# Forgetting heads' values as seven half-block products, logits and rotary key beside 256 latent columns, three gate pairs ahead

## The chip, the cores and the metric

One core of a Trainium2 chip runs the kernel. The metric is the device time of one execution in microseconds (us). Engines: TensorE (PE) for matmuls, VectorE (DVE), ScalarE (ACT), GpSimd (POOL) and SyncE (SP); SP and POOL also issue the DMA transfers, each into its own queue.

## The reference

512 tokens, width 2048, 16 heads of width 128, one input projection of 6472 columns. Cut to what matters:

```
h = _rms_norm(x, g_pre)
q_lat, kv_lat, k_rope_raw, gate_mla, fq, fk, fv, f_logit, gate_fox = split(h @ w_in)
# widths 768, 512, 64, 1024, 1024, 1024, 1024, 8, 1024
o_mla = _mla_branch(rms(q_lat) @ w_uq, rms(kv_lat) @ w_ukv, rope(k_rope_raw)) * silu(gate_mla)
# forgetting heads: c = cumsum(log_sigmoid(f_logit + b_forget))
# logits = q k^T * scale + c_q - c_k, causal softmax, times fv
o_fox = _fox_branch(fq, fk, fv, f_logit, b_forget) * silu(gate_fox)
return x + _rms_norm(concatenate([o_mla, o_fox]) @ w_out, g_post)
```

`fv` is the value projection (1024 columns, 8 heads), `f_logit` the forget logits (8 columns), `k_rope_raw` the rotary key (64 columns), and `q_lat` with `kv_lat` the latents (1280 columns).

## The kernel before

**Numbers.** Each operand is split into a high and a low part, and `mm3` (L139) makes a product of three matmuls: high by high, high by low, low by high. x normalised and transposed lies in SBUF as 16 k-tiles of 128 rows (`hh`, `hl`; `h0` to `h15` in the trace). Weights come in chunks of up to 128 x 1024, loaded by SP (`load`, tile `raw`); `divide` (L255) lets ScalarE make `whi` and VectorE `wlo`, always two chunks ahead of TensorE; the load of a chunk is issued four ahead (`chunk`, L275). Three `raw`, three `whi` and three `wlo` buffers rotate.

**Stages in order.** The list of chunks sets the order.
1. `proj_first` transposes x and multiplies each k-tile at once, with 456 columns: the values of three forgetting heads, 8 logits, 64 of the rotary key.
2. Four pairs of forgetting heads: for pair p the queries `fq`, keys `fk`, (pairs 1 and 2) the values `fv`, and the gates `fg`, each 256 columns: 96 matmuls of 512 tokens with the weights stationary (`proj_T`), while values have the tokens stationary and the weight columns moving (`proj_V`). Pair 1 makes two heads' values (256 wide), pair 2 three (384 wide). `todo` is a list of small steps (attention blocks, fetches); each k-tile of a projection runs one (`pump`). Scores of a pair run beside its gates, values beside the next pair's queries.
3. `lat`: the last 256 latent columns, 96 matmuls of 512.
4. The other 1024 latent columns (group "l") and the 1024 gate columns of the latent heads (group "m"), each as seven products of half blocks (`p1`, `p2`, `p4`, `q6`, `g5`, `g7`, `g3`; 8 k-tiles, 48 matmuls of 512) in place of eight.
5. The latent heads in four pairs ("MLA"), then the output product, again in seven products per half ("o").

**What the half-block products need.** (a) Sums of weight blocks (`t7`, `t6`, `t4`, `t5`), made in DRAM by the DMA engines: `add_step` copies the first block (SP) and adds the second with an accumulating DMA (POOL). `paced` does one step for every so many k-tiles (`pace` 6; a step is 512 KB copied and 512 KB added). A step starts once a mark, written from a weight tile in use, has landed. A late sum (`t4` of l and m, `t5` of o) is not made: its second block is loaded beside the first (`second`) and added by VectorE in `join` (L248). (b) Sums and differences of x's two halves: `x_steps` (L997) adds high and low part (`xr`), `away_steps` (L900) subtracts (`rmg`) and POOL writes the results to DRAM; `fetches` reads them back, `divisions` splits them. These x steps run in `later`, one in three k-tiles, from pair 1 on.

## Time and profile before

| | |
|---|---|
| median of 3 runs | 908.48 us (908.34 to 908.54) |
| the profiled execution, and its span | 905.47 us, 903.7 us |
| TensorE, VectorE, ScalarE, POOL busy | 99%, 70%, 48%, 8% |
| moved by DMA | 195.20 MB, mean 216 GB/s |
| DMA queues: q1 (loads by SP), q0 (POOL) | 55.0% and 20.6% of 16 engines |

Busy time of TensorE counts pipelined matmuls, each modelled as longer than the distance to the next one, so the distances matter more than the 99%. In the row of 40 slices one slice is 22.6 us. In the timeline's rows stand start, duration, engine, tile, line and operation; in the rows of waits tile and line, what released it, total us, count, mean us; in rows of groups the busy time, mean ns of one, and idle time before.

### The profile page before, as it was taken

Reading aid. Unit: us, or ns where it says so; the run is one execution under the profiler, and the core shown is the slowest. Engines: PE = TensorE matmul, PEld = TensorE weight load, DVE = VectorE, ACT = ScalarE, POOL = GpSimd, SP = SyncE. Lnnn points to the kernel's source line nnn. Section 1 sums busy time; section 2 is a strip of 40 time slices with the busy share of each in tenths; the row PEclk is TensorE's granted clock in tenths of the full one; section 3 lists DMA queues with packets and bytes.
Section 4 is the critical chain, followed back from the end, with each engine's and each line's share of the span. In section 5 each row is a group of like instructions: output and inputs, shape, how many; then the busy total and the mean of one; then the engine's idle time right before and its main releaser. Section 6 shows DMA issues by size and latency. Waiting matters only on the chain.

```text
span 903.7 us, 12931 instructions
## 1 busy us (share of the span) xinstructions
PE 895.0 (99%) x4730; PEld 773.2 (86%) x4730; DVE 630.6 (70%) x1070; ACT 433.4 (48%) x806; POOL 71.6 (8%) x89
## 2 busy tenths in 40 slices
PE   9999999999999999999999999999999999999996
PEld 8888888898889988888998998888889888888885
DVE  4477778537463684474867778858879895997785
ACT  6772434234222342233456556545565576645383
POOL 1010102110120110111100000000100000000021
PEclk9999999999999999999999999999999999999999
DMA  9377988987897798988998865247863146798878
GB/s 304 96 202 195 255 203 203 242 228 186 232 262 200 193 245 221 235 218 207 335 396 307 276 212 164 59 109 187 175 171 118 48 139 205 244 320 322 253 222 250
DMA packets 120195, 195.20 MB, mean 216 GB/s; under 512 B 15906, under 2 KB 59452, under 8 KB 120132
## 3 DMA queue, kind: packets, MB, share of 16 engines
q1 hardware_dynamic: 106052, 158.84, 55.0%
q0 software_dynamic: 13344, 35.13, 20.6%
q8 instruction: 37, 0.61, 0.3%
q10 hardware_dynamic: 736, 0.40, 0.2%
q14 instruction: 26, 0.21, 0.1%
HBM read 182.27 MB, written 62.41 MB: 271 GB/s over the span
## 4 chain that ended last, share of the span: by engine, by line
PE 95%; DMA 2%; DVE 1%; ACT 0%; issue 0%; SPq 0%; ACTq 0%; DVEq 0%
PE fv L581 4%; PE fg L140 3%; PE fq L142 3%; PE fq L140 3%; PE fq L141 3%; PE fg L142 3%; PE fg L141 3%; PE fk L141 3%; PE fk L140 3%; PE fk L142 3%; PE sm L624 3%; PE fv L140 2%; PE fv L142 2%; PE fv L141 2%; PE mq L140 2%; PE mq L142 2%
## 5 line engine op out<-in xcount | busy, mean ns | idle before, releaser
L265 DVE TENSOR_TENSOR wlo<-raw,whi 128x1024 fp32r<-128x1024 f32 (+3 forms) x205 | 242.4, 1186 | 157.7 <-ACT whi L262 154.2
L262 ACT CAST whi<-raw 128x1024 fp32r<-128x1024 f32 (+3 forms) x205 | 208.9, 1022 | 287.1 <-PE fk L141 52.9
L140 PE MATMUL fq<-h,whi 128*128 128x512 f32 x128 | 52.6, 411 | 0.0
L140 PE MATMUL fg<-h,whi 128*128 128x512 f32 x128 | 50.9, 398 | 0.0
L142 PE MATMUL fq<-h,wlo 128*128 128x512 f32 x128 | 50.4, 393 | 0.0
L141 PE MATMUL fq<-h,whi 128*128 128x512 f32 x128 | 50.1, 392 | 0.0
L142 PE MATMUL fg<-h,wlo 128*128 128x512 f32 x128 | 50.1, 391 | 0.0
L140 PE MATMUL fk<-h,whi 128*128 128x512 f32 x128 | 50.0, 391 | 0.0
L141 PE MATMUL fg<-h,whi 128*128 128x512 f32 x128 | 49.9, 390 | 0.0
L142 PE MATMUL fk<-h,wlo 128*128 128x512 f32 x128 | 49.8, 389 | 0.0
L141 PE MATMUL fk<-h,whi 128*128 128x512 f32 x128 | 49.8, 389 | 0.0
L142 PE MATMUL fv<-whi,h 128*128 128x256 f32 (+1 forms) x128 | 39.5, 309 | 0.0
L141 PE MATMUL fv<-wlo,h 128*128 128x256 f32 (+1 forms) x128 | 39.5, 309 | 0.0
L140 PE MATMUL fv<-whi,h 128*128 128x256 f32 (+1 forms) x128 | 39.5, 309 | 0.0
L581 PE MATMUL fv<-whi,h 128*128 128x456 f32 x128 | 38.0, 380 | 0.0
L314 POOL DMA_DIRECT2D t<-t x16 | 13.4, 836 | 303.2 <-DMA t<-in_w_out_dram 266.5
L646 ACT ACTIVATE pf<-sf,stf 128x128 f32<-128x128 f32 (+3 forms) x32 | 16.9, 529 | 26.9 <-DVE stf L639 26.9
L140 PE MATMUL mq<-ln,whi 128*128 128x512 f32 x72 | 29.0, 402 | 0.0
L142 PEld LDWEIGHTS fq<-h,wlo 128*128 128x128 f32 x128 | 24.0, 188 | 5.4
L142 PEld LDWEIGHTS fg<-h,wlo 128*128 128x128 f32 x128 | 24.0, 188 | 5.3
L142 PEld LDWEIGHTS fk<-h,wlo 128*128 128x128 f32 x128 | 24.0, 188 | 5.0
L140 PEld LDWEIGHTS fk<-h,whi 128*128 128x128 f32 x128 | 24.0, 188 | 4.9
(519 smaller groups left out, 2471.2 us busy)
## 6 DMA issues: line engine op xcount, KB each, us to landing
raw<-in_w_in_dram SPq DMA_DIRECT2D x80, 512.0 KB
raw<-in_w_out_dram SPq DMA_DIRECT2D x32, 512.0 KB
t<-in_w_out_dram SPq DMA_DIRECT2D x24, 512.0 KB
raw<-t SPq DMA_DIRECT2D x24, 512.0 KB
t<-t POOLq DMA_DIRECT2D x16, 512.0 KB, 7.8
awaymg<-rmg POOLq DMA_DIRECT2D x8, 512.0 KB, 8.0
t<-in_w_out_dram POOLq DMA_DIRECT2D x8, 512.0 KB, 8.2
raw<-t6l SPq DMA_DIRECT2D x8, 512.0 KB
```

Source lines behind the costliest of these rows:

```text
L140: pe.matmul(o, ah, bh, start=first, stop=False, **kw)
L141: pe.matmul(o, ah, bl, start=False, stop=False, **kw)
L142: pe.matmul(o, al, bh, start=False, stop=last, **kw)
L262: cast = act.copy(hi[:, :m], raw[:, :m])
L265: dve.tensor_tensor(out=lo[:, :m], in0=raw[:, :m], in1=hi[:, :m].bitcast(F32), op=ALU.subtract)
L314: pool.dma_start(to.rearrange("p (k c) -> p k c", k=2), second, accum_op=ALU.add)
L581: pe.matmul(banks[t][:, :n], a[k][:, tss[t]], b[:, j, :], start=k == 0 and m == 0, stop=k == NK - 1 and m == 2,)
L624: pe.matmul(s[:, :nn], a[:, qs], c[:, :nn], start=(i == 0), stop=(i == len(pairs) - 1))
L646: act.activation(p, s[:, :n], AF.Exp, bias=st[:, 0:1], scale=unit, accum_out=st[:, 1:2])
```

## The change

1. `proj_first` multiplies 328 columns: the last 256 latent columns, the 64 of the rotary key, the 8 logits. The latent columns are written to DRAM (`l4_away`), fetched after pair 3's scores and transposed (8 transposes); product `lat` goes.
2. The values of all 8 forgetting heads become group "v" of the seven products. `t4` and `t5` of v are late sums (joins on VectorE), `t7` and `t6` eight steps of the planner. Results are combined by `scaled` and `scaled_copy` with the tokens' scale, written to DRAM by POOL (`v_out`, eight writes of half a unit of 512 KB), and fetched and split per pair (`load_v`, `split_v`).
3. The gates of pairs 0, 1 and 2 come ahead: g0, p1, g1, p2, g5, g2, g3, q0, q6, g7, p4, k0, q1, k1, q2, k2, q3, k3, g3 of pair 3. Scores of a pair now run beside the next pair's queries, values beside its keys; the last pair's values beside product `p1` of l.
4. The x steps run right after the first stage as ordinary steps of `todo`; rotary tables and key after the fetched operands of `g5` are split. `later`, `behind`, `proj_V` and `fox_v` go.
5. `pace` is 7 instead of 6; v's sums stand first in the list, then l and m; the output sums are 1024 columns wide (1 MB copied, 1 MB added; 12 steps for 24), and a wide step takes twice the k-tiles. In the latent heads the pace is 1.45 instead of 3. `out_cols` permutes the output's column blocks to fit. `needs` holds at build time that a sum is issued before the chunk that reads it.
6. A pool `vr` (five buffers) holds the blocks of v, two of five `raw` tiles and `second` in this part; `pp` (attention tiles) opens after the block of values; the deep pool of weight buffers, which opened ahead of product `p1` of l, opens after it.

```
-V3 = 3 * HW
+L4 = KVR // 2
+KL = L4 + ROPE
...
     def raw_tile(i):
         if deep and deep[1] <= i < deep[2] and (i - deep[1]) % (DEEP + 3) < DEEP:
             return deep[0].tile([P, 1024], F32, tag="raw", name=f"raw{i}", bufs=DEEP)
+        if i <= prods["p4", "v"][-1] and i % 5 < 2:
+            return vr.tile([P, 1024], F32, tag="raw", name=f"raw{i}", bufs=2)
...
-    state = {"loaded": 0, "divided": 0, "tiles": 0, "turn": 0, "step": -1, "pace": 6}
+    state = {"loaded": 0, "divided": 0, "tiles": 0, "step": -1, "pace": 7}
...
-    fox = []
-    for p in range(4):
-        c = {}
-        if p == 0:
-            c["v"] = add_chunks(
-                w_in, [(0, O_FV + 5 * HW, V3 + NH), (V3 + NH, O_KR, ROPE)], NK, 2, V3 + ROPE + NH, single=2
-            )
-        at = 256 * (3 - p)
-        c["q"] = add_chunks(w_in, [(0, O_FQ + at, 256)], NK, 4, 256)
-        c["k"] = add_chunks(w_in, [(0, O_FK + at, 256)], NK, 4, 256)
-        if p == 1:
-            c["v"] = add_chunks(w_in, [(0, O_FV + 3 * HW, 2 * HW)], NK, 4, 2 * HW)
-        if p == 2:
-            c["v"] = add_chunks(w_in, [(0, O_FV, V3)], NK, 2, V3)
-        c["g"] = add_chunks(w_in, [(0, O_GF + at, 256)], NK, 4, 256)
-        fox.append(c)
-    lat = add_chunks(w_in, [(0, 1024, 256)], NK, 4, 256)
...
-    AT = {"l": 0, "m": O_GM}
+    AT = {"v": O_FV, "l": 0, "m": O_GM}
...
-    for g in "lm":
-        sum_blocks(g, lambda j, h, c, g=g: in_block(g, j, h, c), "t4")
+    for g in "vlm":
+        sum_blocks(g, lambda j, h, c, g=g: in_block(g, j, h, c), ("t4", "t5") if g == "v" else ("t4",))
...
+    first = add_chunks(w_in, [(0, O_KR - L4, KL), (KL, O_F, NH)], NK, 2, KL + NH, single=2)
+    fox = [{} for _ in range(4)]
+    for n in ("g0", "p1", "g1", "p2", "s5", "g2", "s3", "q0", "s6", "s7", "p4", "k0",
+              "q1", "k1", "q2", "k2", "q3", "k3", "g3"):
+        name = {"p1": "p1", "p2": "p2", "p4": "p4", "s5": "g5", "s3": "g3", "s6": "q6", "s7": "g7"}.get(n)
...
+    sum_blocks("o", lambda j, h, c: out_block((K1, K2)[h][j], slice(1024 * c, 1024 * (c + 1))), ("t5",), 1024)
...
+            wide = 0 <= state["step"] < len(bg) and bg[state["step"]][0].shape[1] > 1024
+            pace = state["pace"] * (1 + wide)
...
+    for j in range(4):
+        todo.extend(x_steps(j))
+    wait(4)
+    todo.extend(fetches("g5", "m"))
+    todo.extend(divisions("g5", "m"))
+    todo.append(lambda: todo.extendleft(reversed([*rotary_tables(), rotary_key])))
+
+    fox_g(0, [att_bank("fg00"), bank("pv", "fg01", 1)])
+    A = two_of(proj_bank, "va")
+    product("p1", "v", x_block(0, 0), A, True, True)
+    pa, pb = v_block("vpa"), v_block("vpb")
+    scaled_copy(pa, A, 0, rcol)
+    scaled_copy(pb, A, 2, rcol)
+    fox_g(1, two_of(proj_bank, "fg1"))
+    product("p2", "v", x_block(1, 0), A, False, True)
+    c11 = v_block("vc11")
+    scaled_copy(c11, A, 0, rcol)
+    v_out(c11, 0, 0)
+    drain()
+    G = two_of(att_bank, "vg")
+    product("g5", "v", operand("g5", "m"), G, True, True)
...
+    B = two_of(proj_bank, "vp4")
+    product("p4", "v", x_block(1, 2), B, True, True)
+    scaled(c21, B, 2, c21, col=rcol)
+    v_out(c21, 1, 0)
...
-    todo.append(rotary_key)
-    set_pace(4)
     lb = [proj_bank(f"l4{i}") for i in range(2)]
-    proj_T(lat, [(lb[i], P, two[i]) for i in range(2)], hh, hl)
-    while later:
-        later.popleft()()
     for i in range(2):
+        for t in range(NT):
+            pe.transpose(lb[i][:, t * P : (t + 1) * P], l4[:, t, i * P : (i + 1) * P], ident)
         latent(8 + i, lb[i])
...
+    set_pace(1000)
+    A, A2 = ([proj_bank(f"g{n}{t}") for t in range(2)] for n in "lm")
+    product("p1", "l", x_wide(0, 0), A, True, True, 2, turned=True)
+    drain()
     heads_room.close()
...
-            set_pace(3)
+            set_pace(1.45)
```

In the rows of the order, tile names carry a running number; `rf`, `fz`, `fw`, `fd` belong to the forget sums, `gf` and `ghf` to the gates, `nk` to the forget keys, `fqt` to the queries.

VectorE, up to the split of the chunk that TensorE needs about 140 matmuls after the first stage; first before:

```order
L748 TENSOR_TENSOR fw_773<-fw_773,fz_772 8x512
L749 TENSOR_SCALAR fd_774<-fw_773 8x512
L750 TENSOR_TENSOR fd_774<-fd_774,fz_772 8x512
L751 TENSOR_TENSOR fw_773<-fw_773,fd_774 8x512
L1022 SCALAR_TENSOR_TENSOR fqt00_893<-fq00_728,rrow_211 128x512
L753 SCALAR_TENSOR_TENSOR fz_772<-fz_772,fw_773 8x512
L1022 SCALAR_TENSOR_TENSOR fqt01_899<-fq01_729,rrow_211 128x512
L754 SCALAR_TENSOR_TENSOR rf_215<-fz_772,fd_774 8x512
L132 TENSOR_TENSOR fq00_895<-fqt00_893,fq00_895 128x384
L132 TENSOR_TENSOR fq01_901<-fqt01_899,fq01_901 128x384
L265 TENSOR_TENSOR wlo15_924<-raw15_830,whi15_923 128x1024
L265 TENSOR_TENSOR wlo16_957<-raw16_862,whi16_956 128x1024
```

and after the change:

```order
L749 SCALAR_TENSOR_TENSOR rf_215<-fz_762,fd_764 8x512
L1000 TENSOR_TENSOR xr01_878<-h3_309 128x512
L1000 TENSOR_TENSOR xr11_879<-h10_483 128x512
L1000 TENSOR_TENSOR xr11_879<-h11_515 128x512
L692 SCALAR_TENSOR_TENSOR ghf6_905<-fg00_718,rrow_211 128x512
L692 SCALAR_TENSOR_TENSOR ghf7_909<-fg01_719,rrow_211 128x512
L272 TENSOR_TENSOR wlo15_918<-raw15_826,whi15_917 128x1024
L914 TENSOR_TENSOR rmg51_927<-xr01_878,xr11_879 128x512
L694 SCALAR_TENSOR_TENSOR gf0_904<-gf0_904,ghf6_905 128x512
L694 SCALAR_TENSOR_TENSOR gf0_904<-gf0_904,ghf7_909 128x512
L914 TENSOR_TENSOR rmg51_927<-xr01_878,rmg51_927 128x512
L272 TENSOR_TENSOR wlo16_941<-raw16_866,whi16_940 128x1024
```

The x sums (`xr`, `rmg`) now stand among the splits of the chunks.

TensorE at the third chunk of the product that follows the first one of the list (before: keys of pair 0, after: `p1` of v), before:

```order
L140 MATMUL fk00_919<-h8_418,whi15_923 128x512
L141 MATMUL fk00_919<-h8_418,whi15_923 128x512
L142 MATMUL fk00_919<-h8_418,wlo15_924 128x512
L140 MATMUL fk01_920<-h8_418,whi15_923 128x512
L141 MATMUL fk01_920<-h8_418,whi15_923 128x512
L142 MATMUL fk01_920<-h8_418,wlo15_924 128x512
```

and after:

```order
L142 MATMUL va0_913<-whi15_917,h4_333 128x512
L142 MATMUL va1_914<-whi15_917,h4_333 128x512
L142 MATMUL fg10_1012<-h0_243,whi17_963 128x512
L143 MATMUL fg10_1012<-h0_243,whi17_963 128x512
L142 MATMUL fg11_1013<-h0_243,whi17_963 128x512
L143 MATMUL fg11_1013<-h0_243,whi17_963 128x512
L143 MATMUL va0_913<-wlo15_918,h4_333 128x512
L144 MATMUL va0_913<-whi15_917,h4_333 128x512
L143 MATMUL va1_914<-wlo15_918,h4_333 128x512
L144 MATMUL va1_914<-whi15_917,h4_333 128x512
```

Matmuls that need only `whi`, four of them of the next gates, are pulled ahead of those that need `wlo15`.

SP's queue in the first part, before (`raw` from `in_w_in_dram` are chunks; `t5l`, `t7l` sums of l, of which the 1x16 rows are the marks):

```order
L319 DMA t5l1_118<-whi16_956 1x16
L242 DMA raw19_987<-in_w_in_dram 128x4x256
L317 DMA t5l1_118<-in_w_in_dram 128x2x512
L319 DMA t6l1_110<-whi17_989 1x16
L242 DMA raw20_1017<-in_w_in_dram 128x4x256
L317 DMA t6l1_110<-in_w_in_dram 128x2x512
L242 DMA raw21_1070<-in_w_in_dram 128x4x256
L319 DMA t7l2_107<-whi19_1072 1x16
```

and after, ahead of `g5` (`bmg5` are the fetched x operands, `second` the late blocks):

```order
L232 DMA raw26_1202<-in_w_in_dram 128x2x512
L305 DMA t6v2_111<-in_w_in_dram 128x2x512
L232 DMA raw27_1227<-in_w_in_dram 128x2x512
L928 DMA bmg50_1189<-awaymg50_847 128x512
L928 DMA bmg51_1197<-awaymg51_936 128x512
L928 DMA bmg52_1217<-awaymg52_1035 128x512
L928 DMA bmg53_1225<-awaymg53_1114 128x512
L232 DMA raw28_1252<-in_w_in_dram 128x2x512
L780 DMA pos_1284<-in_positions_dram 128x512
L240 DMA second27_1229<-in_w_in_dram 128x2x512
L249 DMA raw29_1324<-in_w_in_dram 128x4x256
L307 DMA t7v3_108<-whi25_1231 1x16
```

Four fetches and a late block stand between the chunk loads; before there was one load per chunk and a copy for most of them.

More of the change, by code (lines that the diff above doesn't have):

```diff
@@ L209, in tile_hybrid_layer @@
     raws, ready = {}, {}
-    more, deep = [], []
+    more, deep, seconds = [], [], [vr, 2]
+    needs = {}
     def raw_tile(i):
@@ new lines, in split_v, with fox_g @@
+    def split_v(pair, both):
+        values_into(v_pair(f"fv{pair}"), slice(0, 256), [both[:, t, :] for t in range(NT)])
+    gates, gate_slots = {}, {}
+    def fox_g(p, gb):
+        proj_T(fox[p]["g"], [(gb[i], P, two[i]) for i in range(2)], hh, hl)
+        if p == 3:
+            drain()
+        both = gate_slots[p] = slot(f"gf{p}")
+        for i in range(2):
+            h = 2 * (3 - p) + i
+            gates[h] = gate_of(gb[i], both[:, i, :], f"f{h}")
+    v_away = [dr.tile([P, NT * 256], F32, name=f"v_away{i}") for i in range(4)]
@@ new lines, in v_block, with v_out, two_of @@
+    def v_block(name):
+        return vr.tile([P, 2, S], F32, tag="c", name=name)
+    def v_out(c, tokens, half):
+        for i in range(2):
+            to = v_away[2 * half + i].rearrange("p (t c) -> p t c", t=NT)[:, 2 * tokens : 2 * tokens + 2, :]
+            pool.dma_start(to, c[:, :, 256 * i : 256 * (i + 1)])
+    def two_of(make, name):
+        return [make(f"{name}{i}") for i in range(2)]
+    vb = [proj_bank(f"in{t}") for t in range(NT)]
+    with tc.manual_schedule(engines={mybir.EngineType.Activation, mybir.EngineType.DVE, mybir.EngineType.PE}):
+        proj_first(first, vb)
@@ L1293, in tile_hybrid_layer @@
     )
[L1294 to L1296 removed]
+    seconds.extend([deep[0], EXTRA])
+    for j in (1, 0):
+        todo.append(
+            lambda j=j: todo.extendleft(
+                reversed(away_steps("o", j, (o_of[K1[j]], o_of[K2[j]]), ("a11", "a12", "a22")))
+            )
+        )
     pl = slot("lp")
@@ L1533, in done_with @@
             gain(t0 + t, c, o[t], homes.get(t0 + t))
-    assert state["step"] > len(bg) and not later
     gps = [slot(f"gp{c}") for c in range(2)]
```

286 lines of the change are left out of this document (146 added, 140 removed).

## The prediction

> **What bounds the kernel now.** I read the page first: busy shares, slices, queues, chain.
>
> ```profile
> span 903.7 us, 12931 instructions
> PE 895.0 (99%) x4730; PEld 773.2 (86%) x4730; DVE 630.6 (70%) x1070; ACT 433.4 (48%) x806; POOL 71.6 (8%) x89
> PEclk9999999999999999999999999999999999999999
> DMA  9377988987897798988998865247863146798878
> GB/s 304 96 202 195 255 203 203 242 228 186 232 262 200 193 245 221 235 218 207 335 396 307 276 212 164 59 109 187 175 171 118 48 139 205 244 320 322 253 222 250
> q1 hardware_dynamic: 106052, 158.84, 55.0%
> q0 software_dynamic: 13344, 35.13, 20.6%
> PE 95%; DMA 2%; DVE 1%; ACT 0%; issue 0%; SPq 0%; ACTq 0%; DVEq 0%
> ```
>
> TensorE is busy without a break at full clock, and 95% of the chain that ended last is TensorE. Busy alone proves little, since pipelined matmuls overlap, so the next view is what TensorE waited for, over the whole span:
>
> ```profile
> PE mix L1496 <- ACT scaler L1495: 1.9, 1, 1.9
> PE warm L159 <- DVE warm L154: 1.1, 1, 1.1
> PE xt L443 <- DMA xa<-in_x_dram: 0.3, 1, 0.3
> ```
>
> That is 3.3 us. So each matmul removed is worth its pitch (start to start), as long as weights still arrive and are split in time. Pitches come from the timeline of TensorE, two rows of each product, and from the chain for the first stage:
>
> ```profile
> 159.69 0.39 PE L140 MATMUL fk<-h,whi 128*128 128x512 f32 x1
> 171.93 0.39 PE L140 MATMUL fk<-h,whi 128*128 128x512 f32 x1
> ...
> 173.29 0.28 PE L140 MATMUL fv<-whi,h 128*128 128x256 f32 x1
> 178.32 0.28 PE L140 MATMUL fv<-whi,h 128*128 128x256 f32 x1
> ...
> 272.65 0.33 PE L140 MATMUL fv<-whi,h 128*128 128x384 f32 x1
> 281.49 0.33 PE L140 MATMUL fv<-whi,h 128*128 128x384 f32 x1
> ...
> 24.68 0.44 PE xt L443 x4
> 25.12 2.50 PE fv L581 x12
> ```
>
> There are 54, 42 and 51 matmuls from the first to the second of each pair: 12.24/54 = 0.227 us for 512 columns, 5.03/42 = 0.120 for 256, 8.84/51 = 0.173 for 384. The first stage shows 2.50/12 = 0.208 for 456, and four transposes take 0.44.
>
> **TensorE's part.** Removed: 192 matmuls of 456 (40.0 us), 192 of 256 (23.0), 192 of 384 (33.3), and the 96 of 512 that made the last 256 latent columns (21.8): 118.1. Added: 192 matmuls of 328 in the first stage, between the 256 and 384 rows at 0.150, with the first stage's 2% on top 0.153, so 29.4; seven products of 48 matmuls of 512, 336 x 0.227 = 76.2; eight transposes of the stored latent columns, 0.9. Together 106.5. TensorE saves **11.6 us**. The gates, queries, keys and attention are only moved.
>
> **Does the first stage really shrink?** A pair of its k-steps was 5.88 us and would be 2 x (12 x 0.153 + 0.44) = 4.55. ScalarE has to keep up:
>
> ```profile
> L450 ACT ACTIVATE xsq<-xa 128x256 f32<-128x256 f32 x32 | 12.9, 408 | 0.0
> L134 ACT ACTIVATE h<-xt,gcol 128x512 fp32r<-128x512 f32 x15 | 10.2, 688 | 11.7 <-PE xt L443 11.6
> L262 ACT CAST whi<-raw 128x912 fp32r<-128x912 f32 x7 | 6.6, 944 | 0.0
> L262 ACT CAST whi<-raw 128x456 fp32r<-128x456 f32 x2 | 1.1, 562 | 0.0
> ```
>
> Two casts of x (1.4), five squares (2.0) and one weight cast of 656, between the 456 and 912 rows (0.74), are 4.1 us. It fits, with 0.4 to spare, so I count the full shrinking. If it did not fit, at most the stage's 10.6 us would be lost.
>
> **VectorE in the first product.** After the first stage VectorE must make the forget sums, the sums of x's two halves (`xr`, `rmg`, formerly spread over pairs 1 to 3), the first gates, and seven splits of weight chunks, up to the fourth chunk of the first product; the order shown with the change has that last split behind all of these.
>
> ```profile
> L265 DVE TENSOR_TENSOR wlo<-raw,whi 128x1024 fp32r<-128x1024 f32 x176 | 214.4, 1222 | 129.6 <-ACT whi L262 126.5 <-PE gbl L141 1.6 <-PE sm L624 0.5
> L252 DVE TENSOR_TENSOR raw<-raw,second 128x1024 f32<-128x1024 f32 x16 | 19.5, 1219 | 0.2 <-DMA second<-in_w_in_dram 0.2
> L1003 DVE TENSOR_TENSOR xr<-h 128x512 f32<-128x512 f32 x16 | 10.1, 682 | 0.0
> L746 DVE RECIPROCAL fd<-fd 8x512 f32<-8x512 f32 x1 | 3.3, 3344 | 0.0
> L754 DVE TENSOR_TENSOR_SCAN rf<-fz,fd 8x512 f32<-8x512 f32 x1 | 1.2, 1215 | 0.0
> 68.38 0.42 DVE L745 TENSOR_SCALAR fd<-fw 8x512 f32<-8x512 f32 x1
> 53.57 0.86 DVE L472 TENSOR_SCALAR rrowdl<-ident,rrowl 128x128 fp32r<-128x128 f32 x4
> ```
>
> In the order stand 7 splits x 1.22 = 8.5; 26 operations of 512 elements x 0.68 = 17.7; the reciprocal 3.3; the scan 1.2; five of the kind of the 0.42 row, 2.1; and twelve small ones, about 2.9 by the last row: 35.7 us. TensorE gets there after 98 matmuls of the gate, 36 of the product and six pulled ahead, 140 x 0.227, and four transposes: 32.2. So TensorE waits about **3.5 us** there; SP's loads behind it wait too, since a raw buffer is free only after its split. Bounds: 0 if chained rows overlap, 7 if VectorE also stands idle once for ScalarE.
>
> Later in the block VectorE gains 8 joins of late sums (1.2 each), 16 splits of fetched x operands and ten combines, but a gate or query product has a split only every 5.4 us (24 matmuls), so I count nothing. If that cover failed, one join and one split, 2.4 us, would be late per chunk of the two products with late sums.
>
> **The DMA engines in the block of values.** From the first gate to the end of the seventh product TensorE has 4 x 96 + 7 x 48 = 720 matmuls, 163 us. In units of 512 KB the order has in this stretch 49 loads of chunks and late blocks, 10.5 of fetched x operands, keys, positions and values, 16 copies and 16 accumulates for the weight sums (a step for seven k-tiles now, for six before), and 13 plain writes by POOL: 104.5 units, 72.5 plain and 32 of sums. For the prices, three windows (length, busy time of the five engines, granted clock, share of the DMA engines, GB/s) and the issues of the first window:
>
> ```profile
> 53.00:213.00 160.00, 160.00 (x826) 136.80 (x826) 109.80 (x213) 60.58 (x110) 20.71 (x20) 1.00 0.87 217
> 434.00:480.00 46.00, 46.00 (x341) 44.05 (x340) 36.09 (x39) 24.67 (x32) 2.90 (x5) 1.00 1.03 381
> 560.00:720.00 160.00, 159.88 (x867) 137.68 (x866) 130.48 (x254) 87.97 (x195) 6.52 (x7) 1.00 0.50 126
> raw<-in_w_in_dram SPq DMA_DIRECT2D x27, 512.0 KB
> t7l<-in_w_in_dram POOLq DMA_DIRECT2D x4, 512.0 KB, 7.0
> t6m<-t7m POOLq DMA_DIRECT2D x2, 512.0 KB, 5.7
> ```
>
> The second window has nearly only plain transfers and keeps the DMA engines full: 0.524 MB at 381 GB/s with share 1.03 is 1.42 us of all sixteen for a plain unit. The first window is the old pairs: 27 loads, 17 copies by SP's queue, 18 accumulates by POOL's (the last two rows are the first and last of theirs) and 3.5 other plain units. Its 0.87 x 160 = 139 us, less 30.5 x 1.42 = 43.3, leave 96 for 35 units: 2.73 for a unit of sums, which reads memory and writes memory. Note that a full window was fed at share 1.03 and TensorE was busy throughout.
>
> The block: 72.5 x 1.42 + 32 x 2.73 = 190, at share 1.03 185 us, 22 more than TensorE's 163. That is the upper bound of the wait. For the lower one I price accumulates by queue q0's row, 20.6% of 903.7 for 35.13 MB, or 2.78 a unit, and copies as plain: 88.5 x 1.42 + 16 x 2.78 = 170, or 165 us, a wait of 2. Since I trust the window most, there is too much work for the time by it. But loads and sums have different due times. A step comes every seven k-tiles of six matmuls, 7 x 6 x 0.227 = 9.5 us, so the eight v steps take 76 us; in the order the last is issued some 86 us after the first gate starts, and the first product that reads one (`q6`) begins to load it some 125 us after. About 40 us are slack, in which the queue may hold two or three steps; each that runs behind the block gives back 2 x 2.73 = 5.5 us, 11 to 16 in all. 22 less 11 to 16 is 6 to 11 by the window and nothing by the lower price. I take **+4 us**, between the two, nearer the window's; ends 0 and 22.
>
> That sums give way at all is what no row here shows. The Trainium skill ("DMA: Bandwidth & Descriptors", "Queues, rings and completion order") has every DMA engine serve its queue rows in turn, packet by packet; by it sums don't run late but share with the loads, nothing comes back, and the sum would end at the window's 22 us instead of 4.
>
> **What I count as nothing.** The values leave PSUM by copies and POOL writes and come back per pair: in the units above. The deep pool, opened only after the first latent product, lets loads start later there; a late chunk or two would cost 0 to 3 us (two plain units), but TensorE was busy even with the DMA engines full (434:480), so 0. Attention moves one step later, beside the same work. In the last stage ten wide steps (40 half-megabyte transfers) replace seven (14): 26 x 2.73 = 71 us beside the 80 that the third window shows (0.50 x 160), so 151 of 160, nearly full; the sums are first read some 35 us after the last is issued, which is the cover; without it one late sum costs up to 4. 0.
>
> **The sum.** 905.47 - 11.6 + 3.5 + 4 = 901.4 for a profiled run; the runs' median lies 908.48 - 905.47 = 3.0 above it, so **904 us**.
>
> **Rivals.**
> No waits at all: TensorE only gets less to do, 908.48 - 11.6 = 896.9. For it speaks that the 3.3 us of waits in the whole span include none for a weight, although the first slices already show DMA shares of seven to nine tenths; against it that the block asks for more than its time by every price I have. 0.11.
>
> The gain is eaten: the waits come to 10 to 13 us, 906.7 to 910.3, as when the first stage does not shrink because ScalarE has only 0.4 us to spare, or the DMA engines give back less than half. 0.14.
>
> Slower: the DMA engines are oversubscribed in the block of values and nothing is given back. Its place is the products `g5` to `p4`, where a chunk of 12 matmuls, 2.7 us, loads 1.5 to 2.5 units (its weights, in four of the five half a unit of fetched x, in `g5` and `p4` a late block), 2.1 to 3.5 us at 1.42, with the sums and writes on top. Price: 22 there and 3.5 on VectorE, 908.5 - 11.6 + 25.5 = 922.4; it decides once all waits pass 11.6 + 1.8 = 13.4 us. With half given back it is 911 to 917. For it speaks the 0.87 of the first window, against it the slack of 40 us. 0.27.
>
> By another page rule the same rival would be certain: the Trainium skill ("DMA: Bandwidth & Descriptors", "Where 436 GB/s comes from") puts a core's memory traffic at some 358 GB/s. Counting a copy twice and an accumulate three times the block moves 72.5 x 0.524 + 16 x 5 x 0.524 = 80 MB, an estimate of 223 us by that page, 60 beyond TensorE's. But the second window's 381 GB/s stands above that figure already, so the trace does not agree, and I give it no chance of its own.
>
> **How the numbers follow.** The main case, some waiting that leaves most of the saving (899 to 906.5), has 0.48; the others 0.11, 0.14 and 0.27. Less than 0.2%, 1.8 us, I can't tell from no change: the band 906.7 to 910.3 is the third case. So faster 0.59, same 0.14, slower 0.27. From below I leave out nothing but errors of the count, 896; above I leave out the upper part of the slow rival, about 0.1, and stop at 918.
>
> **What the changed profile would show.** Right: 136 fewer matmuls, the first stage's groups of twelve at 1.84 us; TensorE waiting once for `wlo` in the first product, 2 to 5 us, and for some microseconds in all on loads of `raw` or fetched operands between the fourth product and the seventh; DMA slices of nine tenths from about 40 to 200 us, sums late; queue q0's share up from 20.6%. The last stage busier than the third window's 0.50 and still without waits. Wrong: waits of over 13 us on `raw` or `second` in those products (the slow rival), none at all (the fast one), first-stage groups that stay near 2.5 (ScalarE's), waits in the latent products for the late pool or at the output product for a sum, or VectorE's joins ending each chunk in `g5` and `p4`.

## The result, and the profile after

The changed kernel takes 944.03 us (median of 4, 942.73 to 945.45) where the kernel before takes 908.51 (4 runs): ratio 1.0391, 95% interval 1.0371 to 1.0410. It is slower by 35.5 us, where I had forecast 4.5 less. The page of the profiled execution (945.06 us), the lines that answer to those of before:

```profile
span 943.0 us, 12827 instructions
PE 897.2 (95%) x4594; PEld 762.0 (81%) x4594; DVE 674.0 (71%) x1112; ACT 455.8 (48%) x837; POOL 75.1 (8%) x94
PE   9989979999999999999999999997994999999997
PEclk9999979999999999999999999998996999999999
DMA  9678999998998777876899863359999945789878
GB/s 301 176 225 267 303 290 322 298 306 250 279 236 242 185 217 181 234 181 159 282 397 339 264 187 101 99 137 219 226 228 231 226 132 156 246 301 309 280 223 248
q0 software_dynamic: 13552, 41.95, 21.9%
PE 68%; DMA 18%; DVE 8%; ACT 2%; issue 2%; SPq 1%; POOL 0%; ACTq 0%; DVEq 0%; POOLq 0%
```

TensorE does less (136 matmuls fewer), but its row of slices has holes in two places, the third and sixth slice (the block of values) and the 28th and 31st (the latent heads). In three of these slices the row of PEclk shows a lower granted clock. The chain that ended last is now 18% DMA and 8% VectorE. What TensorE waited for, longest first:

```profile
PE pvm L142 <- ACT phm L133: 12.1, 2, 10.3
PE vg L142 <- ACT whi L269: 6.7, 1, 6.7
PE sm L618 <- ACT pm L640: 5.8, 1, 5.8
PE va L143 <- DVE wlo L272: 3.4, 3, 2.7
PE mq L142 <- ACT mw L126: 2.0, 1, 2.0
PE gbl L144 <- DVE wlo L272: 1.8, 4, 0.7
PE vp L143 <- DVE wlo L272: 1.8, 3, 1.0
```

`pvm`, `sm`, `mq` are the latent heads, `va`, `vg`, `vp` products of the values, `gbl` product `p4` of l. Beside the waits stands the clock, first in windows of 20 us (columns as in the prediction), then in the timeline behind the pause of 6.7 us:

```profile
60.00:80.00 20.00, 16.40 (x63) 12.42 (x62) 19.57 (x25) 6.40 (x7) 3.22 (x4) 0.91 0.61 162
120.00:140.00 20.00, 16.95 (x60) 13.19 (x61) 17.29 (x23) 9.47 (x12) 2.68 (x3) 0.77 0.88 286
640.00:660.00 20.00, 14.22 (x63) 11.98 (x62) 9.63 (x26) 7.57 (x21) 0.85 (x1) 0.83 0.91 215
720.00:740.00 20.00, 12.39 (x49) 9.82 (x50) 10.75 (x23) 8.64 (x22) 0.85 (x1) 0.66 0.85 237
```

```profile
122.59 0.79 PE L142 MATMUL vg<-whi,bmg 128*128 128x512 f32 x1 [6.72 <-ACT whi L269]
125.29 0.63 PE L143 MATMUL vg<-wlo,bmg 128*128 128x512 f32 x1
125.72 0.63 PE L144 MATMUL vg<-whi,bmg 128*128 128x512 f32 x1
129.68 0.39 PE L142 MATMUL vg<-whi,bmg 128*128 128x512 f32 x1
129.91 0.39 PE L143 MATMUL vg<-wlo,bmg 128*128 128x512 f32 x1
```

For 6.5 us after the pause a matmul of 512 has a pitch of 0.43 us instead of 0.23.

The next table has the stages of this and later kernels, as times between the first matmuls of products in TensorE's timeline (us; "own" is what TensorE needs without a wait, from the pitches). Each row is the one profiled execution of its kernel. The block's parts are: `p1` and the second gates; `p2` up to the start of `g5`; `g5`, from its first matmul to its last; from there to the last matmul of `p4`, less the key matmuls pulled ahead of it. "Pairs" go on to product `p1` of l, "l" from there to product `q6` of l, "heads" are the latent heads' stage.

| kernel | p1, g1 | p2 | g5 | to end of p4 | pairs | l | heads | span |
|---|---|---|---|---|---|---|---|---|
| own, or before | 32.6 | 10.9 | 10.7 | 87.5 | 209.0 | 73.4 | 131.0 | 903.7 |
| after | 39.6 | 17.8 | 14.6 | 92.7 | 209.0 | 76.3 | 156.5 | 943.0 |
| no_out_sums | 40.3 | 14.7 | 14.6 | 92.0 | 209.0 | 76.4 | 131.0 | 915.1 |
| narrow | 39.6 | 16.9 | 14.6 | 92.9 | 209.0 | 75.9 | 145.4 | 931.8 |
| x_by_act | 34.9 | 17.5 | 14.6 | 92.7 | 209.0 | 76.0 | 157.0 | 938.3 |
| x_out_by_act | 39.6 | 11.4 | 14.5 | 91.7 | 209.0 | 76.0 | 155.3 | 934.0 |
| late_forget | 32.6 | 13.4 | 16.6 | 93.3 | 209.0 | 75.8 | 157.7 | 935.8 |
| late_both | 32.6 | 12.0 | 15.6 | 95.6 | 218.9 | 75.9 | 158.4 | 944.8 |
| early | 39.6 | 17.2 | 14.6 | 93.2 | 214.2 | 76.4 | 133.8 | 925.3 |
| fix1 | 32.6 | 11.0 | 15.3 | 94.7 | 219.7 | 75.8 | 133.2 | 918.2 |
| fix2nj | 32.6 | 10.9 | 15.1 | 94.5 | 219.4 | 75.9 | 131.0 | 915.6 |
| fix2 | 32.6 | 11.0 | 14.0 | 97.1 | 213.9 | 75.8 | 131.0 | 913.3 |
| fix3 | 32.6 | 10.9 | 15.9 | 92.4 | 221.0 | 73.5 | 131.0 | 913.7 |
| fix4 | 32.6 | 10.9 | 16.2 | 93.7 | 213.8 | 73.4 | 131.1 | 908.4 |
| fix5 | 32.6 | 14.1 | 17.4 | 90.7 | 213.7 | 73.4 | 131.0 | 910.7 |

("Own" for pairs and l, which the change composes anew, is the least of these kernels. The later ones order the block otherwise.) Against a kernel that only does TensorE's smaller work, 903.7 - 11.6 = 892.1, the change loses 7.0 + 6.9 + 3.9 + 5.2 = 23 us in the block of values, 2.9 in l and 25.5 in the latent heads. That is the whole of its 51.

### The profile page after: what moved, and what is told of

It reads as the page before. It is cut to its first block, busy times and chain, and to the rows that moved or that the text cites. A ratio compares the mean times of both kernels' runs of the same rounds, so it can differ in the third digit from the quotient of the medians.

```text
span 943.0 us, 12827 instructions
## 1 busy us (share of the span) xinstructions
PE 897.2 (95%) x4594; PEld 762.0 (81%) x4594; DVE 674.0 (71%) x1112; ACT 455.8 (48%) x837; POOL 75.1 (8%) x94
## 2 busy tenths in 40 slices
DMA packets 127259, 223.50 MB, mean 237 GB/s; under 512 B 16570, under 2 KB 53972, under 8 KB 126172
## 4 chain that ended last, share of the span: by engine, by line
PE 68%; DMA 18%; DVE 8%; ACT 2%; issue 2%; SPq 1%; POOL 0%; ACTq 0%; DVEq 0%; POOLq 0%
DMA raw<-in_w_ukv_dram 4%; PE fk L142 3%; PE fk L144 3%; PE fq L142 3%; PE fk L143 3%; PE fq L144 3%; PE fq L143 3%; PE in L575 3%; DVE wlo L272 3%; DMA bmg<-awaymg 2%; DMA t6o<-in_w_out_dram 2%; PE sm L618 2%; DMA second<-in_w_in_dram 2%; PE oa L144 2%; PE oa L143 2%
## 5 line engine op out<-in xcount | busy, mean ns | idle before, releaser
L272 DVE TENSOR_TENSOR wlo<-raw,whi 128x1024 fp32r<-128x1024 f32 (+3 forms) x217 | 256.8, 1187 | 132.5 <-ACT whi L269 129.8
L269 ACT CAST whi<-raw 128x1024 fp32r<-128x1024 f32 (+3 forms) x217 | 220.9, 1023 | 261.9 <-DVE raw L259 33.6
L142 PE MATMUL fk<-h,whi 128*128 128x512 f32 x128 | 52.5, 411 | 0.2 <-ACT whi L269 0.2
L142 PE MATMUL fq<-h,whi 128*128 128x512 f32 x128 | 50.7, 396 | 0.0
L143 PE MATMUL fk<-h,whi 128*128 128x512 f32 x128 | 50.1, 391 | 0.0
L143 PE MATMUL fq<-h,whi 128*128 128x512 f32 x128 | 49.9, 390 | 0.0
L142 PE MATMUL mq<-ln,whi 128*128 128x512 f32 x72 | 30.2, 420 | 2.0 <-ACT mw L126 2.0
L259 DVE TENSOR_TENSOR raw<-raw,second 128x1024 f32<-128x1024 f32 x24 | 29.2, 1218 | 2.8 <-DMA second<-in_w_in_dram 2.8
L575 PE MATMUL in<-whi,h 128*128 128x328 f32 x128 | 29.8, 320 | 0.0
L143 PE MATMUL mq<-ln,whi 128*128 128x512 f32 x72 | 29.2, 405 | 0.0
L144 PE MATMUL mq<-ln,wlo 128*128 128x512 f32 x72 | 29.0, 403 | 0.0
L142 PEld LDWEIGHTS fg<-h,whi 128*128 128x128 f32 x128 | 24.0, 188 | 5.8 <-ACT whi L269 1.1
```

The lines of the kernel that those rows point to most:

```text
L142: pe.matmul(o, ah, bh, start=first, stop=False, **kw)
L143: pe.matmul(o, ah, bl, start=False, stop=False, **kw)
L144: pe.matmul(o, al, bh, start=False, stop=last, **kw)
L259: tc.keep_in_program_order(dve.tensor_tensor(out=raw, in0=raw, in1=second, op=ALU.add))
L269: cast = act.copy(hi[:, :m], raw[:, :m])
L272: dve.tensor_tensor(out=lo[:, :m], in0=raw[:, :m], in1=hi[:, :m].bitcast(F32), op=ALU.subtract)
```

## The experiments

Each ratio is to the kernel before, timed beside it on the same chip.

**Where the 25 us in the latent heads come from.** `no_out_sums`:

```
+    made_o = 2
...
+    del bg[len(bg) - 12 + made_o :]      # ten output sums not made, plain blocks read instead
```

> Leaves out ten of the twelve wide output sums (the products read plain blocks of the output weights instead), so no sums are made in the latent heads' stage; its output is not the layer's. That stage took 156.5 us after the change and 131.0 before. Theory (the sums placed there delay the weight loads): the stage returns to 131 to 133 us and the time to 918 to 921. Rival (something else grew there, such as the attention's order or the gates that come earlier): the stage stays at 150 or more and the time at 940 to 945.

918.27 us, ratio 1.0125 (1.0110 to 1.0141); heads 131.0, their waits gone from the list. Shown: the sums placed there are the cause, and nothing else grew. `narrow`:

```
-    sum_blocks("o", ..., ("t5",), 1024)
+    for g in range(2):
+        sum_blocks(g, lambda j, h, c, g=g: out_block((K1, K2)[h][j], out_cols(2 * g + c)), ("t5",))
```

> The output sums are made in 24 steps of 512 KB instead of 12 of 1 MB, each at half the distance: the same bytes in the same stretch. If the megabyte copies that stand ahead of the weight loads in SP's queue are the cause (order), loads land in 8 to 10 us instead of 15 to 18, TensorE's two long waits in the latent heads mostly go and the time is 925 to 932. If the DMA engines are simply full there (capacity), it stays at 940 to 946.

930.90 us, ratio 1.0264 (1.0236 to 1.0292); heads 145.4. Halving the width of the steps takes back 11 of the 25 us. The time lies in the range that I had named for order, but one of the two long waits stays (7.4 of 10.3 us), so both theories were half right. How it happens shows in the chain of the changed kernel (start, us, what):

```profile
631.74 15.02 DMA raw<-in_w_ukv_dram
...
670.67 5.22 DMA t6o<-whi
675.91 18.03 DMA t6o<-in_w_out_dram
...
695.93 10.39 DMA t7o<-whi
706.39 0.56 SPq L305
...
710.75 18.26 DMA raw<-in_w_ukv_dram
729.06 0.83 ACT whi L269
```

A copy of 1 MB takes 18 us to land, and a mark of 64 bytes 5 to 10. The next copy stands in SP's queue until its mark has landed, and so does what stands behind that copy: four fetches of operands for the output product (`boa`, L928), then key and value weights, which need 15 to 18 us themselves. SP's waits for marks in this stage, after the change (600 to 760 us, two of three rows) and, last, before it (596 to 726 us):

```profile
SPq L305 <- DMA t7o<-whi: 17.5, 3, 6.7
SPq L305 <- DMA t6o<-whi: 11.5, 2, 8.4
SPq L317 <- DMA t<-whi: 7.6, 5, 3.6
```

In ScalarE's timeline the softmax stands behind casts that wait for these loads:

```profile
646.86 1.04 ACT L269 CAST whi<-raw 128x1024 fp32r<-128x1024 f32 x1 [6.75 <-DMA raw<-in_w_ukv_dram]
717.76 0.62 ACT L133 CAST boa<-boa 128x512 fp32r<-128x512 f32 x1 [10.12 <-DMA boa<-awayoa]
722.81 0.62 ACT L133 CAST boa<-boa 128x512 fp32r<-128x512 f32 x1 [4.43 <-DMA boa<-awayoa]
723.34 0.47 ACT L133 CAST phm<-ptm 128x384 fp32r<-128x384 f32 x1
```

The wait of 5.8 us for `pm` is that of the weights. TensorE's longest one, 10.3 us, ended with the cast of `phm` at 723.34, which stood behind two casts of late `boa`; the weights that landed at 729.01 held up only a last wait of 1.8 us. ScalarE's waits for `boa` are 17.3 us in all, 13.8 in `narrow`, and none before the change or in `early`. With narrow steps the chain has one such load of weights, and it is shorter:

```profile
631.32 9.42 DMA raw<-in_w_ukv_dram
```

`early`:

```
     seconds.clear()
+    set_pace(5)          # in the changed kernel: 7 up to product p1 of l
     v_room.close()
...
+    set_pace(6)          # ahead of product q6 of m; in the changed kernel: no steps there
-            set_pace(1.45)
+            set_pace(2.6)
```

> The pace is 5 in the four pairs after the block of values, 6 beside the gate products of the latent heads, 2.6 in the latent heads: 20 sum steps instead of 18 by the end of the pairs with 4 of them wide, 7 by the start of the latent heads, 5 left for them instead of 10. The same sums at another time; nothing is left out. Theory (too many sums in too short a stretch): the latent heads' stage takes 132 to 137 us instead of 156.5, the pairs stay at 211, and the time is 19 to 24 us less than the change. Rival (the wide copies' place ahead of the loads decides, not their number): 142 to 150 us there. If the pairs are as full as the price of 2.73 us per unit says, they lose 2 to 8 us of it.

926.10 us, ratio 1.0207 (1.0178 to 1.0237), 18 us less than the change where I expected 19 to 24. Heads 133.8, as the first theory had it, and the pairs pay 5.2 for it. So it is the number of sums in a short stretch, made worse by their width.

**The block of values.** `x_by_act`:

```
-            dve.tensor_tensor(out=pair[h][:, i, :], in0=hh[k]..., in1=hl[k]..., op=ALU.add)
+            act.copy(pair[h][:, i, :], hh[k].bitcast(F32))
```

> The 16 sums of x's high and low part are replaced by ScalarE copies of the high part (the low part is left out), so VectorE has 16 x 0.68 = 11 us less to do between the first stage and g5. Theory (VectorE is late in the first product): the 6.9 us lost between the start of p1 and the start of p2 shrink to 1 to 2, and as x's operands leave earlier too, the wait of 6.7 us at g5 shrinks: 930 to 938. Rival (the DMA engines bound the block of values whatever VectorE does): the waits move on and the time is 941 to 946.

939.56 us, ratio 1.0357 (1.0338 to 1.0377), above my 930 to 938. The first product loses 2.3 instead of 7.0, but the wait at `g5` stays at 6.4: one half of the expectation held. `x_out_by_act`:

```
-            pool.dma_start(to.rearrange("p (h c) -> p h c", c=HALF), src)
+            (act if of == "m" else pool).dma_start(...)
```

> The eight writes of x's half sums are issued by ScalarE's queue instead of POOL's, where an accumulate that waits for its copy stands ahead of them. Theory (order in POOL's queue): the wait of 6.7 us before g5 and the 3.2 us of slow clock behind it go, 933 to 937. Rival (the DMA engines are full, or the sums themselves are late): the fetch of x lands as late as before and the time is 942 to 946. ScalarE may be held up by VectorE at these issues, which would show as a wait for whi in p1.

937.51 us, ratio 1.0343 (1.0326 to 1.0360), just above my 933 to 937. From the start of `p2` to `g5` it takes 11.4 instead of 17.8: the wait was that of POOL's queue. In the changed kernel's timeline of POOL, and then in its chain, an accumulate waits 8.6 us for its copy, and two writes of x stand behind it:

```profile
101.41 1.21 POOL L302 DMA_DIRECT2D t7v<-in_w_in_dram  x1 [8.57 <-DMA t7v<-in_w_in_dram]
102.15 1.60 POOL L904 DMA_DIRECT2D awaymg<-rmg  x2
```

```profile
102.15 10.98 DMA awaymg<-rmg
113.15 7.80 DMA bmg<-awaymg
```

The clock behind `g5` is full now, yet `g5` still takes 14.5: a second limit had lain under the slow clock. `late_forget`:

```
-    todo.append(lambda: forget_sums(rft))        # ahead of x_steps
...
     todo.extend([*fetches("g3", "m"), *divisions("g3", "m")])
+    todo.append(lambda: forget_sums(rft))
```

> The forget sums (some 11 us of VectorE's work, a reciprocal of 3.3 among it) run after the operands of g3 are split instead of right behind the first stage; nothing is left out. Theory (VectorE has too much to do between the first stage and p2): from the start of p1 to the start of p2 34 to 36 us instead of 39.6, and x's operands leave earlier, so 4 to 8 us less than the change. Rival (the DMA engines bound the block): the waits move to g5, and the time is that of the change within 2 us.

936.08 us, ratio 1.0304 (1.0282 to 1.0325), 8 us less than the change. (In this kernel the rotary key is computed ahead of the rows that it needs, so its output is not the layer's; the same instructions run.) The first product is at TensorE's own 32.6: VectorE's order was the whole of its 7.0. `late_both` moves the rotary work as well:

```
     todo.extend(divisions("g5", "m"))
-    todo.append(lambda: todo.extendleft(reversed([*rotary_tables(), rotary_key])))
...
     heads = None
+    todo.append(lambda: todo.extendleft(reversed([*rotary_tables(), rotary_key])))
     for p in range(4):
```

> As before, and the rotary tables and key (some 20 operations of VectorE), which ran in g5 and g3 between the joins and splits, run beside the first keys instead. Theory (in g5 VectorE has a join and a split for every 2.7 us, and anything else is late): g5 takes 11 to 13 us instead of 14.6 and the whole 8 to 13 us less than the change. Rival (g5 is long because its weights and late blocks land late): g5 stays at 14 to 15 and the time is that of the run with late forget sums alone.

945.46 us, ratio 1.0413 (1.0390 to 1.0435): a miss. `g5` gained 1.0, and the rotary work now stands ahead of the first scores, in the waits of `fix1`, which joins the edits of `late_both`, `early` and `x_out_by_act`:

> Late forget sums, late rotary tables, sums at the early paces, and x's half sums issued by ScalarE's queue, together. If the parts add up, 4 to 6 of the first product, 6 to 10 around g5, 20 to 24 in the latent heads go: 30 to 40 us less than the change, that is from 4 us above the kernel before to 6 below. Rival (the waits are one shortage of the DMA engines, pushed from place to place): 15 to 25 us less than the change, slower than before.

```profile
PE sf L618 <- ACT fw L126: 6.5, 1, 6.5
PE vg L143 <- DVE wlo L272: 3.7, 5, 1.0
PE vp L143 <- DVE wlo L272: 2.2, 3, 1.2
```

919.87 us, ratio 1.0135 (1.0116 to 1.0154). That is 24 us less than the change: the range of the rival, not the 30 to 40 of parts that add up. The pairs take 10.7 us more than in the change, 6.5 of them a wait at the scores (`sf`), and `g5` and `p4` wait for `wlo`.

**Repairs.** `fix2nj` spreads the rotary work over the four key products (six steps each, some now kept in program order) and takes paces 6, 5 and 2.2; `fix2` also joins two chunks ahead; `fix3` also puts `p2` of l ahead of `p4` of l; `fix4` also makes the output sums narrow (the edit of `narrow`).

```
+            turns.extend([*rotary_tables(), rotary_key])                       # fix2nj, at p == 0
+        todo.extendleft(reversed([turns.popleft() for _ in range(min(len(turns), 6))]))
         k = fox_k(p, wholes)
...
-        for k in range(i + ahead + 1, min(state["loaded"], i + ahead + (3 if deep else 2))):
+        for k in range(i + ahead + 1, min(state["loaded"], i + ahead + (3 if deep or seconds else 2))):    # fix2
             join(k)
...
-            ("p1", "l"), ("p1", "m"), ("p4", "l"), ("p2", "l"), ...
+            ("p1", "l"), ("p1", "m"), ("p2", "l"), ("p4", "l"), ...            # fix3
```

> Forget sums late, rotary tables in six pieces beside the four key products, paces 6, 5 and 2.2 (34, 37 and then the rest of 44 steps), x's half sums issued by ScalarE. Against the run with all fixes so far the pairs should return from 221.9 to 212 to 216 us (6.5 of it was a wait of the first scores behind the rotary work, the rest sums) and the latent heads stay at 132 to 137: 5 to 10 us less, 909 to 914. If the pairs stay at 220, the rotary work was not the cause.

> The same, and in the block of values the late block is joined two chunks ahead of its split instead of one. Theory (join, cast and split of one chunk follow one another, 1.22 + 1.05 + 1.22 us and hand-overs, some 3.7, against 2.72 of matmuls): g5 goes from 15 to 11.5 to 12.5 us and p4 loses 1 to 2, 3 to 6 us less than without. Rival (VectorE is simply full in g5): no change there.

> The same as the last, with product p2 of l ahead of p4 of l, so that the late blocks of p4, loaded only when the deep pool is open, have 11 us more. Theory: the 2.8 us lost between p4 of l and q6 of l go. Rival (join and split bind there too): 0 to 1 us.

> The same as the last, with the output sums in 24 steps of 512 KB and a pace of 1.9 in the latent heads. With few sums left there the width should matter little: within 2 us of the last one; if the order ahead of the loads matters, 2 to 4 us less.

915.89 (ratio 1.0080, 1.0057 to 1.0103), 915.72 (1.0093, 1.0061 to 1.0124), 915.21 (1.0076, 1.0061 to 1.0091), 912.57 (1.0056, 1.0040 to 1.0073). The 6.5 us at the scores went, but the pairs stayed at 219.4 in `fix2nj`, with new waits of 5.3 us in the attention's values and slow clock behind them: there the expectation failed. From 213.8 to 221.0 the pairs now vary from profile to profile, but the edits need not be the reason: `fix2` and `fix3` have 213.9 and 221.0, and what tells them apart is an order behind the pairs; the executions of `fix2` alone lie between 911.94 and 920.12 us. l is 2.4 us shorter with `p4` later, as expected. The narrow sums of `fix4` left the heads where they were (131.0 and 131.1), so its 2.6 us are not explained by them. Joining earlier did little: `g5` 14.0 to 16.2. In `fix4` a row of VectorE in `g5` waits for a late block:

```profile
111.85 1.22 DVE L259 TENSOR_TENSOR raw<-raw,second 128x1024 f32<-128x1024 f32 x1 [1.91 <-DMA second<-in_w_in_dram]
```

Three more try to take that apart: late blocks in general slots (`fix5`), the gates of pair 2 ahead of `g5` (`fix7`), both (`fix6`).

```
-    more, deep, seconds = [], [], [vr, 2]
+    more, deep, seconds = [], [], []                  # fix5, fix6: slot() instead
...
-    for n in ("g0", "p1", "g1", "p2", "s5", "g2", "s3", ...
+    for n in ("g0", "p1", "g1", "p2", "g2", "s5", "s3", ...    # fix7, fix6
```

> As the last one, and the late blocks of the values lie in the general slots instead of two buffers of their own, so that their loads need not wait for a join. Theory (in g5 and p4 the late block's load is issued only when a buffer is free and lands 10 us later): g5 goes from 16.2 to 12 to 13.5 us and p4 loses 1 to 2, together 3 to 6 us less, 907 to 909.5. Rival (VectorE's own work bounds g5, or slots are short and something else waits): 911 to 914.

> As the run with narrow output sums, and the gates of pair 2 stand ahead of g5 instead of behind it, so that the fetch and split of x's operands have 21.8 us more and only joins and splits are left in g5; late blocks in their two buffers. Theory (g5 is late because three things of VectorE and two of the DMA queue fall on it at once): 11.5 to 14 us for g5, but g3 follows it directly and its own operands have only g5's time: 908 to 912. Rival (the two buffers decide): g5 stays at 15 to 16 and g3 loses besides, 912 to 917.

> Both: gates of pair 2 ahead of g5, late blocks in general slots. If both theories hold, 905 to 908, the first to be faster than the kernel before; if g3's operands are late now, 909 to 913.

913.14 (1.0064, 1.0040 to 1.0088), 916.28 (1.0091, 1.0070 to 1.0111), 912.82 (1.0050, 1.0031 to 1.0069): three misses, each in the slower of its two ranges. More buffers alone gave nothing in `g5`; `p4` reached its own 10.9, but the wait in front of `g5` came back with 3.2. In `fix5` VectorE is busy for 13.8 of the 21.4 us around `g5`, waits 6.1 us there for late blocks, and ScalarE waits 9.8 for the fetched x: landings have a part in it, not VectorE's work alone. With the gates moved `g5` was no longer late, but `g3`, now directly behind it, waited 6.3 and 4.0 us until VectorE had taken `g5`'s result out of the banks that `g3` adds to. So something long has to stand between them: `fix8` puts the queries of pair 0 there, and half the rotary work into the gaps between score blocks; `fix9` has other paces, and `fix10` paces between the two, the positions loaded early and less rotary work beside the first keys. (The three calls of `set_pace` are put on one line here.)

```
-    for n in ("g0", "p1", "g1", "p2", "s5", "g2", "s3", "q0", "s6", ...
+    for n in ("g0", "p1", "g1", "p2", "g2", "s5", "q0", "s3", "s6", ...
...
+                todo.append(turns.popleft() if turns and b % 2 else lambda: None)    # behind each h.scores(b)
...
-    set_pace(6), set_pace(5), set_pace(1.9)           # fix8, as in fix4: pairs, gates, heads
+    set_pace(7), set_pace(4), set_pace(1.7)           # fix9
+    set_pace(6.7), set_pace(5), set_pace(1.75)        # fix10
```

> As the run with the gates of pair 2 ahead of g5 and late blocks in general slots, with the queries of pair 0 between g5 and g3 (so that VectorE can take g5's result out of PSUM before g3 adds to it, and g3's operands have 21.8 us), and the rotary work half beside the first keys and half in the gaps between score blocks. Theory (each of g5 and g3 is late only when its VectorE work falls on it at once): g5 11 to 12.5 us, g3 10.9 to 12, the block of values 2 to 5 us over TensorE's own time, the pairs 211 to 214: 904 to 908, at or below the kernel before. Rival (q6's operands, fetched beside g3, are late instead, or the DMA engines now bind): 909 to 914.

> The same with paces 7, 4 and 1.7, so 34 of 56 half-megabyte steps by the end of the pairs instead of 37, and 9 instead of 7 beside the latent heads' gates. If sums in the pairs delay the values that are fetched there, the pairs lose 1 to 3 us less and the time is 1 to 3 us lower; if not, the same within 1.

> As the run with the queries of pair 0 between g5 and g3, with the positions loaded before product p4 (their load landed 12 us late and VectorE's queue stood behind it: 2.3 us at the first scores), less rotary work beside the first keys, and paces 6.7, 5 and 1.75 (35 steps by the end of the pairs, 42 by the latent heads). If the two runs before show the two ends of one trade (pairs 215.5 and 210.9 us, latent heads 131.4 and 135.8), a middle pace gets 211 to 213 and 131 to 132.5, and with the positions early the time is 3 to 6 us less than the kernel before, 902 to 905. If the sums cost the same wherever they lie, it stays at 906 to 909.

907.73 (ratio 1.0006, 0.9992 to 1.0021), 909.36 (1.0022, 1.0003 to 1.0041), 906.91 (1.0000, 0.9977 to 1.0022). `fix8` is inside its range; `fix9` is 1.6 us more than `fix8`, where I expected 1 to 3 less or the same; `fix10` lies in the range named for sums that cost the same wherever they lie, not in 902 to 905. `g5` takes 10.65 us in all three, TensorE's own. Pairs and heads: 215.8 and 131.4, 211.1 and 135.8, 209.6 and 131.9. In these three profiles the sums don't cost the same everywhere, but each is one execution, and those of one kernel spread by 6 to 12 us, so this stays open. The profiled execution of `fix10` (903.05 us, span 901.3) has these waits, and these windows (block of values, latent heads):

```profile
PE vg L143 <- DVE wlo L272: 2.1, 2, 1.5
PE mix L1564 <- ACT scaler L1563: 1.9, 1, 1.9
PE vp L143 <- DVE wlo L272: 0.8, 1, 0.8
```

```profile
44.00:214.00 170.00, 166.33 (x730) 135.42 (x729) 123.21 (x158) 69.30 (x92) 21.56 (x23) 1.00 0.99 307
591.00:723.00 132.00, 131.40 (x749) 114.71 (x748) 107.85 (x217) 74.44 (x184) 14.33 (x15) 1.00 0.83 206
```

Its executions spread from 900.81 to 913.18 us, those of the kernel before on that chip from 904.77 to 909.69. The repairs win back the whole loss, but no version beat the kernel before; what the other executions of `fix10` wait for was not seen.

## Why the prediction was wrong

**TensorE's part: right.** The first gates start at 42.29 us where the first queries started at 53.04, 10.75 earlier for 10.6 in the sum. A step of the first stage, first matmul to transpose to first matmul, is 2.24 us for 2.28:

```profile
18.94 0.40 PE L575 MATMUL in<-whi,h 128*128 128x328 f32 x1
20.82 0.60 PE L462 MATMUL xt<-ident,xa 128*128 128x128 f32 x4
21.18 0.40 PE L575 MATMUL in<-whi,h 128*128 128x328 f32 x1
```

**VectorE in the first product: right mechanism, 7.0 instead of 3.5**, the upper bound; 5.1 of it are waits and 1.9 a slow clock behind them. Its seventh split ended at 81.5 us, 39.2 after the first gates' start at 42.3 and not 35.7: the work was counted rightly, but VectorE stood idle in it, as its waits from 42 to 82 us show, for the two functions that ScalarE computes in the forget sums and for TensorE's transposes. The bound allowed for it ("stands idle once for ScalarE"), the sum did not. And behind the pause of 2.7 us TensorE ran 3.4 us at half clock.

```profile
DVE fw L739 <- ACT fw L736: 2.1, 1, 2.1
DVE rf L730 <- PE rf L729: 1.1, 1, 1.1
DVE fw L735 <- ACT fz L733: 0.7, 1, 0.7
```

**The DMA engines in the block: 16 us (6.9 + 3.9 + 5.2) instead of 4, and mostly by another mechanism.** `fix10` moves its block in 170 us at a share of 0.99, 5.6 over TensorE's own, so the lower bound (165 us, a wait of 2) was nearer. 0.99 x 170 less the 71 plain units that it issues there at 1.42 leaves 2.2 us for each of its 31 units of sums, where I had 2.73. What cost was order: POOL's queue (6.3, by `x_out_by_act`) and the step "a gate or query product has a split only every 5.4 us, so I count nothing", which was about the wrong products. In `g5` itself joins, splits of fetched x and, in the changed kernel, rotary work come together (`late_forget`: 5.9 over its own 10.7). With the gates of pair 2 ahead of it `g5` loses nothing (`fix8`); whether VectorE's queue or the landings of its operands set the 5.9 is not separated.

**The deep pool: 2.9 where I took 0 (0 to 3).** The late blocks of `p4`; `fix3` took 2.4 back.

**The last stage: 25.5 where I took 0 (0 to 4). This step failed the forecast.** The load itself was less than I had added up: from 574 to 759 us, the stretch that answers to 560:720 before, the DMA engines' share is 0.75, so 139 us for my 151. I called it hidden because "the sums are first read some 35 us after the last is issued, which is the cover". But that covers the sums only. The weights and fetched operands of the same stage go through the queue in which the copies stand and wait for their marks, and they were late: TensorE waited 12.1 + 5.8 + 2.0 us, and slow clock came on top. Without the sums the stage takes 131.0, with steps half as wide 145.4, with half as many of them 133.8. I had asked when the sums are wanted, not who stands behind them. The stage has three buffers for its weights, where the deep pool of 434:480, beside which TensorE was busy with full DMA engines, has six more; that more buffers would help in the heads was not run.

**No term at all for the clock.** After pauses of 2.7, 6.7, 5.8 and 10.3 us TensorE's matmuls ran at a pitch of 0.43; by what they took beyond their pitch these four stretches cost some 8 to 10 us, an estimate (1.9 and 3.2 in the block of values, the rest in the heads). A pause of 0.8 had no such stretch. Over all the runs here every pause of 3.05 us and more had one, while of those between 1.75 and 2.76 some had one and some had not: at the same place the pause of 2.68 in the changed kernel did, one of 2.69 in `narrow` did not. The Trainium skill ("TensorE: Matmul & The Clock Gate", "Part 1: The HAM clock gate") says that the array falls to half clock after an idle window of some 3.4 us and needs as long a busy one to return; the trace agrees with the half clock and, at 3.4 to 6.5 us in the block of values, roughly with the return, while the pause of 2.7 us was shorter than the window that it names.

The slower rival had 0.27 and 922. It had the direction right, but it lay in the block, where not even half of the loss was, and rested on full DMA engines, which cost at most 5.6 us there in `fix10`.

## What to carry to other kernels

Spare DMA time only hides a transfer if the loads in the same queue are far enough ahead: name what stands behind each instruction that waits in a queue (a copy behind its mark, a write behind an accumulate), on the queue that issues and on the engine that waits for what lands. Counting the buffers between a load and its user should help too; no run here shows that by itself. When a change moves side work from a long, even stretch into a short one, price each engine's queue chunk by chunk in the product where it lands, and add the slow clock to every pause of more than 3 us; from 1.8 us on it may come. Less work on TensorE is worth its time only where the others have room: here 11.6 us less of it took 43 us more of VectorE's (630.6 to 674.0) and 28 MB more of DMA (195.20 to 223.50).

## What the runs showed of the hardware

Half a clock after a pause (0.43 instead of 0.23 us, for 3.4 to 6.5 us) can hide a second limit: in `g5` the splits of the weights (`wlo`) were as late as the slow matmuls, so taking the pause away left `g5` at 14.5 us. And nearly full DMA engines and a busy TensorE go together for 170 us in `fix10` (share 0.99, 307 GB/s, copies and accumulates among it, 5.6 us over TensorE's own). In its latent heads a share of 0.83 cost 1 us, with half-megabyte steps and 27 MB, while 0.84 with megabyte copies ahead of the loads, and 32 MB, went with 25 us lost in the changed kernel:

```profile
610.00:765.00 155.00, 135.17 (x738) 116.66 (x738) 106.91 (x214) 73.31 (x183) 9.39 (x10) 0.92 0.84 204
```
